# The keys' low part over all 128 rows of the array in the attention scores

## The chip, the cores and the metric

The kernel runs on one core of one Trainium2 chip. The metric is the device time of one execution in microseconds (us); the time before is 1739.68 us, the median of three runs (1738.67 to 1740.33). The engines are named as in the profile: PE multiplies matrices, PEld is its weight load (it loads the stationary operand, and overlaps PE), DVE is the vector engine, ACT the scalar engine, POOL the general-purpose engine, SP the engine that issues most transfers.

## The reference

The model is a two-layer transformer for 256 tokens of an image (a 4 by 64 grid) and 256 tokens of context, 1024 features, float32. Each layer has a half feed-forward, an attention block and a second half feed-forward, all modulated by a condition. The change lies in the attention's scores:

```
s_lat = einsum('bjqhd,bjykhd->bhjqyk', q_r, k_blk) * scale      # neighbourhood, 4 heads of 64
s_ctx = einsum('bjqhd,bchd->bhjqc', q_r, k_ctx) * scale         # the same queries on the context
p = softmax(concatenate([s_lat, s_ctx]))
...
s = einsum('bqkgd,bskd->bkgqs', q, k) * (64 ** -0.5)            # grouped heads: 8 of queries, 2 of keys
p = softmax(s); o = einsum('bkgqs,bskd->bqkgd', p, v)
```

In the first layer the context's tokens have their own queries, and attend to the context alone; in the second layer they only give keys and values.

## The kernel before, in words

All large products keep float32 accuracy by splitting each operand into a high part (float32r, which PE takes at its fast rate) and a low part, the remainder. `mm3` (L348, L349, L350) issues three matmuls for one product: high by high, high by low, low by high. These three lines are most of the program. Weights arrive by SP into `raw` buffers, ACT casts the high part (L306), DVE subtracts for the low part (L309), and both go into a buffer `w` of the pool `wp`, of which there are 7.

The order of all work is written out by hand: the kernel is traced under a manual schedule, and each engine runs its instructions in the order in which the code emits them. `later` and `tick` postpone small steps until so many microseconds of matmuls have been emitted. Buffers of a pool are handed out as earlier tiles are done with, and the framework adds the waits.

In `attention`, softmax goes by *units*. A unit is two heads: in a unit of kind "x", a block of 128 image tokens over all 512 keys; in a unit of kind "c", all 256 context tokens over the 256 context keys. The first layer has 4 + 8 units x and 2 + 4 units c (neighbourhood and grouped heads), the second 4 + 8 units x. `run` emits for each unit its scores, then dense matmuls that are independent of it (the amounts are in the table `FILL`), then the transposes of the unit two places earlier (`flip`, L878 and L883), so that DVE and ACT have time for the maximum (L855), the exponentials (L863) and the copies (L886).

A head has 64 features, and the array 128 rows, so the three terms of a score are packed into two matmuls. The queries' tile of two heads holds, for head i, the high part on that head's half of the rows and the low part on the other half. The keys' tile `K`, a buffer of the pool `wp`, has four planes of 512 columns: planes 0 and 1 are the high parts of heads 0 and 1, each on both halves of the rows; plane 2 has both low parts, head i on its half; plane 3 has the neighbourhood queries of the image tokens, in the spare room. The first matmul of a score (L838) is queries by high keys over all 128 rows, which sums two of the terms. The second (L839) is the third term, the queries' high part by the keys' low part, and uses only the 64 rows of head i:

```
PE.matmul(out=o, lhsT=q[:, i, tt * 128:(tt + 1) * 128], rhs=kt[:, i, keys], start=True, stop=False)
PE.matmul(out=o, lhsT=q[r, i, tt * 128:(tt + 1) * 128], rhs=kt[r, 2, keys], start=False, stop=True)
```

A unit x thus has four matmuls of 512 columns, which alternate between L838 and L839; a unit c has eight of 256 columns. `key_tile` allocates a tile K: two for the neighbourhood heads at the start of a layer's attention, one for the grouped heads before the third unit. `split_keys` fills it (ACT L710, DVE L713), `split_queries` fills the queries (ACT L724 or L721, DVE L725 or L722). The queries of later units lie in tiles `qst` of the pool tag `t2k`, of which there are 12; the probabilities `P`, the squares `qsq` and the pooling's matrices `pmd` share them. POOL does little here: the rotation's product (L736), and for the next layer a memset of `bm` and `pwbd` (L644, L645) and some gathers (L660).

Of the kernel before, what the change touches and what calls it, by code (L numbers as in the profile page):

```python
# [9 lines left out]
F32 = mybir.dt.float32  # L10
# [8 lines left out]
TX = 256  # L19
# [31 lines left out]
def dit_kernel(  # L51
# [123 lines left out]
    def ada_quantum(g, k, raw):  # L175
        """128 rows of two of the modulations, by the tensor engine."""
        if k == 0:
            ada_ps[g] = ps_ada.tile([128, 512], F32, tag="ada", name="ada")
        ps = ada_ps[g]
        for j in range(4):  # L180
            PE.matmul(out=ps[32 * j:32 * j + 32, :], lhsT=sc[:, k, :], rhs=raw[:, j * 512:(j + 1) * 512], start=(k == 0), stop=(k == KD - 1))  # L181
        st["raws"] -= 1
        loads()
        if k == KD - 1:
            sb = ada_rows(ada_ps.pop(g))
            later(5.0, lambda: ada_columns(sb, [2 * g, 2 * g + 1], 2))
# [3 lines left out]
    def conds(m):  # L190
        """How many conditions a modulation is for: the context's tokens end with the second layer's attention."""
        return 1 if m >= 14 else 2
# [8 lines left out]
    def ada_one():  # L201
        """The next block of the modulations, 128 rows by 512 columns, that the vector engine does: it sums both conditions'
        multiples of the rows; the sums over partitions are the tensor engine's, once for a modulation."""
# [38 lines left out]
    def ada_columns(sb, ms, n):  # L242
        """Rows 32j (and the one after) of four groups of columns become columns of the modulations ms."""
        tp = aux_bank()
        for q in range(2 * conds(ms[0]) if n == 1 else 4):
            PE.transpose(tp[:, q * 128:(q + 1) * 128], sb[:, q * 128:(q + 1) * 128], ident)
        tv = tp.rearrange("p (q j w) -> p q j w", q=4, j=4)
        for i, m in enumerate(ms):
            l, mod = divmod(m, 9)
            s = conds(m) if n == 1 else 2  # L250
            sl = modT[:, l * 72 + mod * 8:l * 72 + mod * 8 + 8, 0:s]
            if n == 1:
                v, o = tv[:, 0:2 * s, :, 0].rearrange("p (s q) j -> p j q s", s=s), sl.rearrange("p (j q) s -> p j q s", j=4)
            else:
                v, o = tv[:, :, 2 * i:2 * i + 2, 0:2].rearrange("p q j s -> p j q s"), sl.rearrange("p (j q) s -> p j q s", j=2)
            bsrc = (colsB if l else colsA)[:, mod * 8:mod * 8 + 8].rearrange("p (j q) -> p j q", j=o.shape[1])
            DVE.tensor_tensor(out=o, in0=v, in1=bsrc[:, :, :, None].to_broadcast(list(o.shape)), op=ALU.add)
            derived(l, mod, s)
# [12 lines left out]
    def next_main(force=False):  # L271
        """Whether the next weight block of the stream is on its way; ada blocks before it go to the tensor engine."""
# [7 lines left out]
    def run_ada():  # L280
        """Runs the next ada block of the stream, if that is what comes next."""
# [9 lines left out]
    def emit_split(between=None):  # L291
        """Splits the next slot of the stream into two float32r parts (ada blocks on the way go to the tensor engine)."""
# [51 lines left out]
    def mm3(ps, pairs, n, start, stop):  # L344
        """Accumulates products of split operands: pairs of ((wh, wl), (ah, al)); the first of each is stationary."""
# [17 lines left out]
    def acc_chunk(vs, k):  # L363
        """Squares of chunk k of the halves vs of the tokens; summed over chunks, but a half's last chunk apart."""
# [18 lines left out]
    def rsqrt(ps, n, scale):  # L383
        """1 / sqrt(ps * scale + EPS) of few elements, by Newton's steps from a guess at the exponent."""
# [27 lines left out]
    def spread(v, rb=None):  # L412
        """The tokens' factors on every partition."""
# [5 lines left out]
    def apply(v, i, a, pace=0.0, rb=None):  # L419
        """The operand of the next product: normed, scaled and shifted, in two parts."""  # L420
# [45 lines left out]
    def proj_out(src, kl, ppair, gate, both, final, after, each=None):  # L466
        """One part of a product into the residual. src(k) gives the moving operand; a slot has ppair chunks. In the final
        part the last two slots go by halves of the tokens, so that one half's norm runs under the other."""
# [35 lines left out]
    def boundary(i):  # L504
        """What follows a finished half: its statistic and its operand of the next product."""
# [26 lines left out]
    def by_halves(sl, a, both, evac):  # L532
        """Products of four slots, one half of the tokens after the other, chunk by chunk of the operand as it comes. Two
        products share a bank: the first start clears what the whole bank has had written."""
# [11 lines left out]
    def up_evac(pa, pb, g, m, nm, lo, hi):  # L546
        """g[m : m + nm] of the tokens lo:hi from the banks of both factors."""
# [89 lines left out]
    def attn_prep(l):  # L637
        """Bias of the neighbourhood's scores (masked), and the pooling weights as blocks of a diagonal."""
# [11 lines left out]
        # copies of a head's table at a pitch of 465, read back at a pitch of 464: row c starts c entries earlier  # L650
# [24 lines left out]
    def attention(l, a, both):  # L675
        """From the normed tokens to the operand of w_out and the first half of that product; both: the context's tokens
        are carried on too."""
# [20 lines left out]
        # k of the neighbourhood, k and v of the grouped heads: by halves of the tokens  # L698
        sl = [take() for _ in range(4)]

        def key_tile():
            """Keys of two heads: each one's high part on both halves of the rows, then both low parts; and some queries."""
            st["out"] += 1
            return wp.tile([128, 4, 512], F32R, tag="w", name="K")
        K = {("na", hp): key_tile() for hp in range(2)}

        def split_keys(kt, src, lo, hi):
# [3 lines left out]
            for i in range(2):  # L711
                r = slice(64 * i, 64 * i + 64)
                DVE.tensor_tensor(out=kt[r, 2, lo:hi], in0=src[r], in1=kt[r, i, lo:hi].bitcast(F32), op=ALU.subtract)  # L713

        def split_queries(dst, src, scale=None):
            """Queries of two heads, each one's high part on its half of the rows and its low part on the other."""
# [10 lines left out]
        def rotate(q, n):  # L727
            """Rotary embedding of n chunks of the first TX tokens in place."""
# [15 lines left out]
        def k_post():  # L744
            """Norm and rotation of the grouped heads' keys."""
# [29 lines left out]
        # q and v of the neighbourhood  # L775
        Q = {}
        for j in range(2):
# [3 lines left out]
            for v in halves(both):  # L781
                if v:
                    q = tmp.tile([128, 512], F32R, tag="t2k", bufs=T2K, name="qst")
                else:
                    q = K["na", j][:, 3]
# [18 lines left out]
        # the pooling's matrices: each block of tokens on itself; on its neighbour they are in k_edge  # L804
# [9 lines left out]
        def queries(br, kind, hs):  # L814
            """Both heads' queries as they are multiplied."""
# [7 lines left out]
        def scores(br, kind, hs, t):  # L823
            """x: one block of 128 tokens over all keys; c: all of the context's tokens over its keys."""
# [9 lines left out]
            for tt in ((t,) if br == "x" else (0, 1)):  # L834
                for i in range(2):
                    r = slice(64 * i, 64 * i + 64)
                    o = S[i] if br == "x" else S[i][:, tt * TX:(tt + 1) * TX]
                    PE.matmul(out=o, lhsT=q[:, i, tt * 128:(tt + 1) * 128], rhs=kt[:, i, keys], start=True, stop=False)  # L838
                    PE.matmul(out=o, lhsT=q[r, i, tt * 128:(tt + 1) * 128], rhs=kt[r, 2, keys], start=False, stop=True)  # L839
# [27 lines left out]
        def flip(br, kind, hs, t, Ps):  # L867
            """Probabilities with the keys on partitions; the products with v once a pair of heads has them all."""
# [59 lines left out]
        def run(jobs, fill, before):  # L928
            """Units of softmax, each one's probabilities turned depth units later."""
# [19 lines left out]
        def stat_col(c, tb):  # L949
            """Where the statistics of chunk c's two heads lie, for a block of tokens."""  # L950
            return c // 2 * nb * 4 + tb * 4 + c % 2 * 2

        def q_post(j):
            """Rotation and norm of two chunks of queries."""
# [9 lines left out]
        def rest_in():  # L964
            """q of the grouped heads and u of the pooling."""
# [27 lines left out]
        def rest_out():  # L993
            """The product with w_out's first half: the neighbourhood's and the pooling's chunks."""
# [53 lines left out]
        def piece():  # L1048
            """A piece of the work that is independent of the units."""
# [21 lines left out]
        def before(n):  # L1071
            """What the unit n needs, beyond its queries."""
# [40 lines left out]
    with tc.manual_schedule():  # L1113
        # small operands, laid in rows and turned into columns
# [13 lines left out]
        def quarter_load(h, i, raw):  # L1128
            """Half of the rows of the first shift's and scale's chunks 2h and 2h + 1."""
# [19 lines left out]
        def load_pair(v, k2):  # L1149
            """Two chunks of half the tokens, turned."""  # L1150
# [7 lines left out]
        def quarter_ada(h):  # L1158
            """The products of two chunks of the shift and scale: each of the array's four groups of columns sums a quarter of
            the rows."""  # L1160
# [25 lines left out]
        # sums of squares of the tokens as they come, a token on a partition  # L1186
# [27 lines left out]
        def first():  # L1214
            """The first four slots' products, as the shift and scale and with them the operand's chunks come."""
# [45 lines left out]
        def last_chunk(ch):  # L1261
            """A chunk of the result, scaled by the last norm's gains."""
# [20 lines left out]
        # final norm of the tokens, which are back in rows  # L1283
# [16 lines left out]
def _constants():  # L1300
    """Arrays that depend on the shapes alone."""
# [55 lines left out]
```

## Time and profile before

| what | value |
|---|---|
| median of 3 runs | 1739.68 us (1738.67 to 1740.33) |
| profiled execution: span from first to last instruction | 1741.7 us |
| PE busy | 1706.1 us, 98% |
| PE weight loads busy | 1428.7 us, 82% |
| DVE, ACT, POOL busy | 1025.0, 664.8, 33.3 us |
| mean granted clock of PE | 0.987 |
| L838 | 48 matmuls of 128x512, 24 of 128x256 |
| L839 | 48 of 64x512, 24 of 64x256 |

The page gives no other time of the profiled execution than its span, which is 2.0 us above the median of the runs. Busy times of PE overlap, because matmuls are pipelined: a matmul's duration is not what it adds to the program. What it adds is the time from its start to the start of the next one, which the timeline gives. Shapes in the rows are written rows*columns of the stationary operand and rows x columns of the moving one: 64*128 64x512 is a matmul that uses 64 rows of the array.

### The profile page before, as it was taken

How to read it: one execution, taken by the hardware profiler on the slowest of the kernel's cores; microseconds unless marked ns; L12 is line 12 of the kernel's file. 1: busy time of each engine (PE TensorE's matmuls, PEld its weight loads, DVE VectorE, ACT ScalarE, POOL GpSimd, SP SyncE). 2: the span in 40 equal slices, each digit the busy share in tenths (PEclk: the TensorE clock that was granted, in tenths of full speed). 3: DMA queues.
4: the chain of work that ended last, by engine and by line, in shares of the span. 5: the costliest groups of instructions: out<-in, count | busy, mean ns of one | idle time of the engine just before them, and what ended most of it. 6: DMA issues, size and time to landing. Idle time of an engine off the chain costs nothing.

```text
span 1741.7 us, 23662 instructions
## 1 busy us (share of the span) xinstructions
PE 1706.1 (98%) x9512; PEld 1428.7 (82%) x9512; DVE 1025.0 (59%) x1748; ACT 664.8 (38%) x1087; POOL 33.3 (2%) x48
## 2 busy tenths in 40 slices
PE   6999999999999999999999999999999999989998
PEld 4778888889886688888888898888888987789998
DVE  5666676566545586666664466545433656565554
ACT  4431322324545644323333243223222356554443
POOL 0000200000000000000000000020000000000000
PEclk8999999999999999999999999999999999989999
DMA  9755555431304325544653335455533133546561
GB/s 316 207 175 168 155 179 173 151 121 49 109 25 160 107 73 168 164 140 140 192 152 122 92 88 183 150 160 174 146 97 97 49 110 146 169 133 205 164 201 50
DMA packets 295335, 246.48 MB, mean 142 GB/s; under 512 B 9377, under 2 KB 262442, under 8 KB 293176
## 3 DMA queue, kind: packets, MB, share of 16 engines
q1 hardware_dynamic: 292680, 241.30, 44.7%
q0 software_dynamic: 1088, 2.15, 0.5%
q8 instruction: 75, 1.23, 0.3%
q10 hardware_dynamic: 1456, 1.52, 0.3%
q14 instruction: 36, 0.29, 0.1%
HBM read 243.88 MB, written 2.00 MB: 141 GB/s over the span
## 4 chain that ended last, share of the span: by engine, by line
PE 90%; DVE 4%; DMA 2%; ACT 2%; issue 1%; SPq 0%; DVEq 0%; ACTq 0%
PE mm L348 27%; PE mm L350 27%; PE mm L349 27%; PE mm L839 2%; PE mm L912 1%; PE aux L878 1%; PE mm L838 1%; DVE w L309 1%; PE ada L181 1%; DMA ada_raw<-in_w_ada_dram 1%; DVE ada_acc L221 1%; PE ada L229 1%; DMA raw<-in_w_ada_dram 1%; ACT w L306 1%; PE aux L409 0%
## 5 line engine op out<-in xcount | busy, mean ns | idle before, releaser
L348 PE MATMUL mm<-act,w 128*128 128x512 f32 (+1 forms) x2592 | 913.0, 352 | 5.6 <-ACT act L437 3.3
L350 PE MATMUL mm<-act,w 128*128 128x512 f32 (+1 forms) x2592 | 904.2, 349 | 1.8 <-DVE w L309 1.8
L349 PE MATMUL mm<-act,w 128*128 128x512 f32 (+1 forms) x2592 | 904.5, 349 | 1.0 <-DVE act L431 0.9
L348 PEld LDWEIGHTS mm<-act,w 128*128 128x128 f32 x2592 | 494.1, 191 | 89.3 <-issue 19.4
L350 PEld LDWEIGHTS mm<-act,w 128*128 128x128 f32 x2592 | 494.0, 191 | 64.1 <-DVE w L309 2.4
L349 PEld LDWEIGHTS mm<-act,w 128*128 128x128 f32 x2592 | 494.3, 191 | 62.5 <-DVE act L431 1.7
L309 DVE TENSOR_TENSOR w<-raw,w 128x1024 fp32r<-128x1024 f32 (+1 forms) x312 | 371.0, 1198 | 245.6 <-ACT w L306 245.2
L306 ACT CAST w<-raw 128x1024 fp32r<-128x1024 f32 (+1 forms) x312 | 314.9, 1023 | 120.4 <-PE mm L350 93.6
L221 DVE SCALAR_TENSOR_TENSOR ada_acc<-ada_raw,sc,ada_acc 128x512 f32<-128x512 f32 x308 | 216.0, 746 | 47.9 <-DMA ada_raw<-in_w_ada_dram 24.7
L558 ACT CAST act<-gf 128x512 fp32r<-128x512 f32 (+1 forms) x87 | 49.7, 571 | 318.7 <-DVE gf L555 318.7
L461 DVE SCALAR_TENSOR_TENSOR hT<-mm,hgt,hT 128x256 f32<-128x256 f32 x168 | 75.1, 480 | 97.8 <-PE mm L350 97.6
L552 ACT ACTIVATE sil<-mm 128x512 f32<-128x512 f32 (+1 forms) x87 | 47.6, 547 | 214.8 <-PE mm L350 214.5
L555 DVE TENSOR_TENSOR gf<-sil,mm 128x512 f32<-128x512 f32 (+1 forms) x87 | 54.3, 625 | 94.0 <-PE mm L350 77.7
L559 DVE TENSOR_TENSOR act<-gf,act 128x512 fp32r<-128x512 f32 (+1 forms) x87 | 54.9, 631 | 55.5 <-ACT act L558 55.5
L374 ACT ACTIVATE sq<-hT 128x256 f32<-128x256 f32 (+1 forms) x52 | 25.5, 492 | 108.4 <-DVE hT L461 108.4
L437 ACT ACTIVATE act<-nt,modT 128x256 fp32r<-128x256 f32 x88 | 43.4, 507 | 49.3 <-DVE nt L436 49.2
L219 ACT ACTIVATE ada_acc<-ada_raw,sc 128x512 f32<-128x512 f32 x44 | 29.6, 718 | 47.4 <-DMA ada_raw<-in_w_ada_dram 36.7
L855 DVE TENSOR_REDUCE nm<-mm 128x1 f32<-128x512 f32 (+1 forms) x60 | 41.0, 686 | 7.9 <-PE mm L839 7.2
L863 ACT ACTIVATE P<-mm,nm,rq 128x512 f32<-128x512 f32 (+1 forms) x48 | 33.7, 707 | 22.3 <-DVE nm L860 21.0
L431 DVE SCALAR_TENSOR_TENSOR act<-nt,modT,act 128x256 fp32r<-128x256 f32 x88 | 41.3, 480 | 1.3 <-ACT act L437 1.3
L436 DVE SCALAR_TENSOR_TENSOR nt<-hT,gsc,aux 128x256 f32<-128x256 f32 x88 | 40.8, 476 | 1.8 <-PE aux L416 1.2
L886 ACT COPY PT<-aux 128x512 f32<-128x512 f32 x60 | 32.2, 588 | 16.9 <-PE aux L878 12.9
(154 smaller groups left out, 885.5 us busy)
## 6 DMA issues: line engine op xcount, KB each, us to landing
raw<-in_ffn_up_dram SPq DMA_DIRECT2D x172, 512.0 KB
ada_raw<-in_w_ada_dram SPq DMA_DIRECT2D x192, 256.0 KB
raw<-in_ffn_down_dram SPq DMA_DIRECT2D x32, 1024.0 KB
raw<-in_w_ada_dram SPq DMA_DIRECT2D x16, 1024.0 KB
raw<-in_ffn_down_dram SPq DMA_DIRECT2D x16, 768.0 KB
raw<-in_w_in_dram SPq DMA_DIRECT2D x10, 1024.0 KB
raw<-in_w_out_dram SPq DMA_DIRECT2D x8, 1024.0 KB
raw<-in_w_ada_dram SPq DMA_DIRECT2D x12, 512.0 KB
```

The costliest lines, as they stand in the source:

```text
L221: DVE.scalar_tensor_tensor(out=o, in0=raw, scalar=col, in1=o, op0=ALU.mult, op1=ALU.add)
L306: ACT.copy(out=wh, in_=sl)
L309: DVE.tensor_tensor(out=wl, in0=sl, in1=wh.bitcast(F32), op=ALU.subtract)
L348: PE.matmul(out=ps, lhsT=wh, rhs=ah, start=start and i == 0, stop=False)
L349: PE.matmul(out=ps, lhsT=wh, rhs=al, start=False, stop=False)
L350: PE.matmul(out=ps, lhsT=wl, rhs=ah, start=False, stop=stop and i == last)
L437: ACT.activation(out=acol(a, k, v * TX, v * TX + TX)[0], in_=t, func=AF.Identity, bias=modT[:, l * 72 + 3 * n * 8 + k, v:v + 1])
L461: DVE.scalar_tensor_tensor(out=hT[:, k, cols], in0=ps, scalar=gate[:, k, v:v + 1], in1=hT[:, k, cols], op0=ALU.mult, op1=ALU.add)
L552: ACT.activation(out=s[:, 0:n], in_=pa[:, 0:n], func=AF.Silu)
L555: DVE.tensor_tensor(out=u[:, 0:n], in0=s[:, 0:n], in1=pb[:, 0:n], op=ALU.mult)
L558: ACT.copy(out=gh, in_=uv)
L559: DVE.tensor_tensor(out=gl, in0=uv, in1=gh.bitcast(F32), op=ALU.subtract)
```

## The change

The keys' low parts get a plane each, planes 2 and 3 of the tile K: head i's low part on its half of the rows, zeros on the other half. The second matmul then runs over all 128 rows with the same stationary operand as the first; the other head's half of the rows holds this head's low queries, which meet zeros. POOL writes the zeros when the tile is allocated, two memsets of 64 rows by 512 columns for each of the three tiles of a layer. Since plane 3 is taken, the image tokens' neighbourhood queries move to tiles `qst` of the tag `t2k`. (The changed file also lost its comments; lines from 705 on are moved by up to four.)

```
         def key_tile():
             st["out"] += 1
-            return wp.tile([128, 4, 512], F32R, tag="w", name="K")
+            kt = wp.tile([128, 4, 512], F32R, tag="w", name="K")
+            for i in range(2):
+                POOL.memset(kt[64 - 64 * i:128 - 64 * i, 2 + i].bitcast(F32), 0.0)
+            return kt
...
                 r = slice(64 * i, 64 * i + 64)
-                DVE.tensor_tensor(out=kt[r, 2, lo:hi], in0=src[r], in1=kt[r, i, lo:hi].bitcast(F32), op=ALU.subtract)
+                DVE.tensor_tensor(out=kt[r, 2 + i, lo:hi], in0=src[r], in1=kt[r, i, lo:hi].bitcast(F32), op=ALU.subtract)
...
             for v in halves(both):
-                if v:
-                    q = tmp.tile([128, 512], F32R, tag="t2k", bufs=T2K, name="qst")
-                else:
-                    q = K["na", j][:, 3]
+                q = tmp.tile([128, 512], F32R, tag="t2k", bufs=T2K, name="qst")
...
-                    r = slice(64 * i, 64 * i + 64)
                     o = S[i] if br == "x" else S[i][:, tt * TX:(tt + 1) * TX]
                     PE.matmul(out=o, lhsT=q[:, i, tt * 128:(tt + 1) * 128], rhs=kt[:, i, keys], start=True, stop=False)
-                    PE.matmul(out=o, lhsT=q[r, i, tt * 128:(tt + 1) * 128], rhs=kt[r, 2, keys], start=False, stop=True)
+                    PE.matmul(out=o, lhsT=q[:, i, tt * 128:(tt + 1) * 128], rhs=kt[:, 2 + i, keys], start=False, stop=True)
```

The order of PE's instructions stays as it was. On PE, at the first unit of the first layer, the two orders differ as follows (rows with - are of before, rows with + of the changed kernel; in brackets stands what the instruction waits for):

```order
-L838 MATMUL mm<-K 128x512 [waits DVE_49,PE_49]
-L839 MATMUL mm<-K 128x512
-L838 MATMUL mm<-K 128x512 [waits Activation_49]
-L839 MATMUL mm<-K 128x512
+L838 MATMUL mm<-K,qst 128x512 [waits DVE_49,PE_49]
+L839 MATMUL mm<-K,qst 128x512 [waits Pool_49]
+L838 MATMUL mm<-K,qst 128x512 [waits Activation_49]
+L839 MATMUL mm<-K,qst 128x512 [waits Pool_49]
```

The queries come from `qst` now, and the first second-matmuls of each tile K wait for POOL's zeros. On POOL, around the first layer's attention and up to the second layer's `bm`, the order before is:

```order
L660 DMA braw<-tab 64x4x64 x16
L736 ISA
L736 TENSOR_TENSOR qkv<-qkv,rope 128x256
L736 TENSOR_TENSOR qkv<-qkv,rope 128x2x256 x2
L644 MEMSET bm 128x2048
```

and after the change, where L707 is the memset of the zeros and L740 the rotation's product of L736:

```order
L660 DMA braw<-tab 64x4x64 x16
L707 MEMSET K 64x512 x4
L740 ISA
L740 TENSOR_TENSOR qkv<-qkv,rope 128x256
L707 MEMSET K 64x512 x2
L740 TENSOR_TENSOR qkv<-qkv,rope 128x2x256 x2
L644 MEMSET bm 128x2048
```

Four memsets stand ahead of the rotation of the keys, and two ahead of the rotations of the queries.

## The prediction

> **What bounds the kernel now.** I read the page first, for the engine that bounds the whole, then the same by stage, then what PE waits for in the stages that the change touches, and last the timeline of single score units.
>
> ```profile
> PE 1706.1 (98%) x9512; PEld 1428.7 (82%) x9512; DVE 1025.0 (59%) x1748; ACT 664.8 (38%) x1087; POOL 33.3 (2%) x48
> PE 90%; DVE 4%; DMA 2%; ACT 2%; issue 1%; SPq 0%; DVEq 0%; ACTq 0%
> ```
>
> PE is busy for 98% of the span and carries 90% of the chain that ended last. The busy share alone is no proof, since matmul durations overlap, so I look at the two stretches that hold the score units, and at PE's waits in them (one answer for each stretch, engine and releaser, us in total, times, longest):
>
> ```profile
> 457.00:610.00 153.00, 152.52 (x880) 107.65 (x878) 78.07 (x192) 86.01 (x200) 4.64 (x4) 0.98 0.28 93
> 1424.00:1508.00 84.00, 83.54 (x582) 60.74 (x581) 51.24 (x122) 53.81 (x115) 2.61 (x2) 1.00 0.42 152
> PE aux L883 <- ACT PT L886: 0.5, 2, 0.2
> PE mm L838 <- ACT P L863: 0.4, 1, 0.4
> ```
>
> The columns of the first two rows are length, then busy time of PE, PEld, DVE, ACT and POOL, granted clock, DMA share and GB/s. In 237 us of units, PE waits 0.9 us. ACT, the next busiest, works 86.01 of 153 us and 53.81 of 84 us. So here a microsecond less on PE is a microsecond less of the program, until ACT or DVE is in the way.
>
> Now the units themselves. These rows are the start, the modelled duration and the shape of PE's matmuls at the first unit, with dense work on both sides:
>
> ```profile
> 457.73 0.40 PE L838 MATMUL mm<-K 128*128 128x512 f32 x1
> 458.06 0.50 PE L839 MATMUL mm<-K 64*128 64x512 f32 x1
> ...
> 459.34 0.50 PE L348 MATMUL mm<-act,w 128*128 128x512 f32 x1
> 459.68 0.40 PE L349 MATMUL mm<-act,w 128*128 128x512 f32 x1
> 459.92 0.40 PE L350 MATMUL mm<-act,w 128*128 128x512 f32 x1
> 460.15 0.40 PE L348 MATMUL mm<-act,w 128*128 128x512 f32 x1
> ```
>
> Between full-row matmuls of 512 columns the next starts 0.23 us later (459.92 to 460.15). Inside the unit, where 128 and 64 rows alternate, the first step takes 0.33 us, the other three 1.28 together (458.06 to 459.34), 0.43 each, and even the step after the return to full rows (459.34 to 459.68) takes 0.34. The weight loads tell why:
>
> ```profile
> 458.91 0.18 PEld L839 LDWEIGHTS mm<-K 64*128 64x128 f32 x1 [0.24 <-issue]
> 459.33 0.19 PEld L348 LDWEIGHTS mm<-act,w 128*128 128x128 f32 x1 [0.24 <-issue]
> 459.92 0.19 PEld L348 LDWEIGHTS mm<-act,w 128*128 128x128 f32 x1
> ```
>
> In the unit the loads start only as their own matmul does (458.91 and 459.33, after 0.24 us of idle), so each step is 0.24 plus 0.18; in the dense stream the load of 459.92 belongs to the matmul of 460.15 and runs beside the one before. Loads of 64 and of 128 rows cost the same, 0.18 and 0.19 us; what the change of the number of rows costs is that they are no longer hidden.
>
> **The change, part by part.** It removes all changes of the number of rows inside a unit. The counts:
>
> ```profile
> L839 PE MATMUL mm<-K,qst 64*128 64x512 f32 x32 | 15.8, 495 | 0.0
> L839 PE MATMUL mm<-K 64*128 64x512 f32 x16 | 7.9, 496 | 0.0
> L839 PE MATMUL mm<-K,qst 64*128 64x256 f32 x24 | 9.1, 381 | 0.0
> ```
>
> That is 48 of 512 columns, two in a unit x: 24 units. And 24 of 256 columns, four in a unit c: 6 units.
>
> *A unit x.* From its first matmul to the one after the return, the first unit takes 459.68 - 457.73 = 1.95 us for five steps. At the dense stream's step these are 5 x 0.23 = 1.15, a gain of 0.80. Most units follow transposes, after which a full-row matmul has one longer step too; its price stands at places where dense work follows transposes, and at another unit:
>
> ```profile
> 507.82 0.48 PE L838 MATMUL mm<-K,qst 128*128 128x512 f32 x1
> 509.51 0.39 PE L348 MATMUL mm<-w,act 128*128 128x256 f32 x1
> 509.74 0.28 PE L349 MATMUL mm<-w,act 128*128 128x256 f32 x1
> 582.77 0.48 PE L348 MATMUL mm<-act,w 128*128 128x512 f32 x1
> 583.09 0.39 PE L349 MATMUL mm<-act,w 128*128 128x512 f32 x1
> 404.39 0.36 PE L348 MATMUL mm<-act,w 128*128 128x256 f32 x1
> 404.59 0.28 PE L349 MATMUL mm<-act,w 128*128 128x256 f32 x1
> 404.71 0.28 PE L350 MATMUL mm<-act,w 128*128 128x256 f32 x1
> ```
>
> Now 509.74 - 507.82 = 1.92; later 0.32 (582.77 to 583.09) + 3 x 0.23 + 0.12 (404.59 to 404.71, the step of 256 columns) = 1.13, a gain of 0.79. I take 0.80 for each: 24 x 0.80 = 19.2 us.
>
> *A unit c* has eight steps and the one after the return:
>
> ```profile
> 489.12 0.36 PE L838 MATMUL mm<-K,qst 128*128 128x256 f32 x1
> 491.60 0.50 PE L348 MATMUL mm<-act,w 128*128 128x512 f32 x1
> 491.94 0.39 PE L349 MATMUL mm<-act,w 128*128 128x512 f32 x1
> ```
>
> Now 491.94 - 489.12 = 2.82; later 0.20 (404.39 to 404.59, after transposes) + 7 x 0.12 + 0.23 = 1.27, a gain of 1.55. Six units: 9.3 us.
>
> *Less* for units that are followed by matmuls of fewer columns (L1015 128*64, L181 128*32), which change the array's shape anyway; there are seven, the first and the last of them:
>
> ```profile
> 529.72 0.50 PE L839 MATMUL mm<-K,qst 64*128 64x512 f32 x1
> 530.15 0.65 PE L1015 MATMUL mm<-pmd,qkv 128*64 128x128 f32 x4
> ...
> 1490.05 1.06 PE L181 MATMUL ada<-raw,sc 128*32 128x512 f32 x8
> 544.10 0.39 PE L350 MATMUL mm<-act,w 128*128 128x512 f32 x1
> 544.42 1.06 PE L181 MATMUL ada<-raw,sc 128*32 128x512 f32 x8
> ```
>
> There the last step goes from 0.43 to 0.32 (544.10 to 544.42), a gain of 0.11 and not 0.20, and the 0.11 after the return isn't had: 7 x 0.2 = 1.4 us less. PE's sum is 19.2 + 9.3 - 1.4 = 27.1 us.
>
> *The zeros.* Twelve memsets of 64x512 on POOL. The nearest rows:
>
> ```profile
> L644 POOL MEMSET bm<- 128x2048 f32 x2 | 3.6, 1824 | 0.0
> L645 POOL MEMSET pwbd<- 128x256 f32 x2 | 0.7, 331 | 34.9 <-issue 34.9
> 436.57 1.73 POOL L736 TENSOR_TENSOR qkv<-qkv,rope 128x256 f32<-128x256 f32 x1 [245.15 <-ACT w L306]
> 480.30 1.30 POOL L736 TENSOR_TENSOR qkv<-qkv,rope 128x512 f32<-128x512 f32 x1 [42.01 <-PE aux L732]
> 468.49 2.51 ACT L710 CAST K<-qkv 64x512 fp32r<-64x512 f32 x4
> ```
>
> Between 0.33 and 1.82 us each; by its length near the first, say 0.6. The neighbourhood's four memsets stand ahead of the rotation of the keys at 436.57, in 245.15 us of POOL's idle time, and their zeros are first read at 457.73, 21 us behind that rotation. The tile of the grouped heads is the same buffer that ACT fills from 468.49 on, so POOL can have its zeros done by 472 at the dearer price, while POOL has 42.01 us of idle time before the rotation at 480.30, and the first unit that reads the zeros starts at 507.82. Cost zero; the cover is that idle time, and without it the rotation of the queries, and with it the grouped heads' units, would come up to 3.6 us later in each layer, two memsets at 1.82.
>
> *The moved queries and low keys* cost ACT and DVE the same instructions into another tile or plane. Two more of the 12 `t2k` tiles are held in each layer until the fourth unit, so later tiles get other buffers, and some instructions wait for other ones. The transposes that free a tile P are emitted two units behind its scores, before the next tile that could need its place, and PE's waits above show no shortage, so I cost this at nothing; the bounds are 0 and what the rival on `t2k` below gives.
>
> *What is late next.* The units come 0.8 us closer, ACT and DVE keep their work. The two waits of 0.9 us in all are ACT's; each can grow by about a unit's gain where ACT is not released earlier. I take 1.5 us off, with ends of 0 and 8 (ten of the second layer's twelve units giving back 0.8 each). The forecast is 27.1 - 1.5 = 25.6 us less: 1716.1 for this execution, whose span is 2.0 above the median of the runs, so 1714 for the median.
>
> **The rivals.** *The load stays exposed.* The second matmul has the same stationary operand as the first, yet would load it again; if a load over all rows couldn't run beside a matmul on the same rows, each step would stay 0.24 + 0.19, as now, and the time 1740. For it: L838 has full rows, and the step from L838 to L839 is as long as the one back. Against it: in the dense stream loads of the same shape do run beside, and L348 and L349 share their stationary operand just so; hence 4 in 100. The Trainium skill's page "TensorE: Matmul & The Clock Gate", section "Part 3: Packing small matmuls — row/col tiling", states this rule: a weight load overlaps matmuls in flight only when the row group differs. By that rule the change would gain nothing, and the dense stream's loads at 0.23 us a step contradict it here.
>
> *Softmax takes over.* In the second layer ACT would work 53.81 of about 75 us, 72%; if half of the gain turned into waits on ACT or DVE, the time would be 1740 - 13 = 1727. Against it stand only 0.9 us of waits now, and transposes two units behind. 8 in 100.
>
> *Slower: the crowded `t2k`.* With two tiles more in use, a new P or `qsq` tile may have to wait for the transposes of an older one, so that ACT stands still and the scores wait for their bank. It decides from 27/30 = 0.9 us a unit on, somewhat more than a unit x gains; at twice its gain, 1.6 us a unit, the time would be 1740 - 27 + 48 = 1761. Against it: the order of all instructions is unchanged, and each buffer is freed by an instruction emitted earlier. 4 in 100.
>
> **How the numbers follow.** The forecast has 84 in 100, with its own range of 1709 (no loss, and 3 us of slow clock less: it was granted at 0.98 in the first stretch) to 1722 (8 us given back). The two rivals beside it, 1727 and 1740, and the slower one hold 16, so the range stays 1709 to 1722. Within 0.2%, 3.5 us, which is about what a measurement can tell from no change, lies only the exposed load: same 0.04. Faster 0.92, slower 0.04.
>
> **What would show it.** Inside a unit L838 and L839 start 0.23 us apart (0.12 in units c), and the first dense step after a unit takes 0.23. The units' lengths fall from 1.60 to about 0.9 and from 2.48 to 1.04 us. POOL has twelve memsets, all long before the units that read them. PE's waits in the two stretches stay under 3 us. It would be wrong if the steps stay at 0.42, if L839 waits for POOL, or if PE's waits on ACT grow by tens of microseconds.

## The result, and the profile after

The changed kernel takes 1719.26 us (median of 4 runs, 1716.95 to 1720.09), the kernel before beside it 1740.01 us (4 runs, 1738.67 to 1741.38): a ratio of 0.9882, with the interval 0.9868 to 0.9896, or 20.7 us less. The forecast was 1714, in the range 1709 to 1722. Run again twice, on two occasions, the changed kernel took 1714.77 and 1715.66 us, against 1738.91 and 1739.68: 24.1 and 24.0 us less. What differs between these sets is how long PE's clock stood at one half; among all runs with a mean granted clock of 0.990 the medians are 1739.7 (12 runs) and 1715.6 (5 runs), with 0.991 they are 1738.7 (15) and 1714.8 (2), and with 0.988, which three of the first set's four runs had, 1742.3 (4) and 1719.3 (4). So at equal clock the change is worth 23 to 24 us.

The profiled execution took 1716.95 us, with a span of 1715.2. First the page's busy times, and its chain of work that ended last:

```profile
PE 1675.8 (98%) x9512; PEld 1420.5 (83%) x9512; DVE 1024.0 (60%) x1748; ACT 663.5 (39%) x1087; POOL 40.0 (2%) x60
PE 90%; DVE 4%; DMA 3%; ACT 2%; issue 1%; SPq 0%; DVEq 0%; ACTq 0%
```

PE issues as many matmuls as before, is busy for 30.3 us less and still bounds the program; POOL has twelve instructions more. Next the table by stretches, for those that hold the score units (start and end, length; busy time of PE, PEld, DVE, ACT, POOL; granted clock, DMA share, GB/s), and PE's waits on ACT and on the modulations' blocks in them (us in total, times, longest):

```profile
457.00:592.00 135.00, 134.21 (x892) 103.25 (x890) 78.97 (x196) 86.27 (x205) 5.71 (x6) 1.00 0.32 106
1403.00:1483.00 80.00, 77.00 (x590) 61.34 (x588) 51.75 (x123) 54.56 (x116) 3.63 (x4) 1.00 0.47 164
PE mm L838 <- ACT P L863: 1.3, 1, 1.3
PE ada L181 <- DMA raw<-in_w_ada_dram: 1.2, 1, 1.2
PE aux L883 <- ACT PT L886: 0.5, 2, 0.2
```

The waits in the units have grown from 0.9 to 3.0 us: a wait of 0.4 on ACT's exponentials has become 1.3, and one of 1.2 us on a transfer is new. Both are in the second layer. (A wait of L246, 0.24 us in both executions, is left out: it lies behind the last unit.) The first unit x and the first unit c by the timeline (start, duration, instruction):

```profile
457.94 0.40 PE L838 MATMUL mm<-K,qst 128*128 128x512 f32 x1
458.17 0.40 PE L839 MATMUL mm<-K,qst 128*128 128x512 f32 x1
458.41 0.39 PE L838 MATMUL mm<-K,qst 128*128 128x512 f32 x1
458.64 0.40 PE L839 MATMUL mm<-K,qst 128*128 128x512 f32 x1
458.87 0.39 PE L348 MATMUL mm<-act,w 128*128 128x512 f32 x1
459.10 0.39 PE L349 MATMUL mm<-act,w 128*128 128x512 f32 x1
...
486.08 0.36 PE L838 MATMUL mm<-K,qst 128*128 128x256 f32 x1
486.28 0.28 PE L839 MATMUL mm<-K,qst 128*128 128x256 f32 x1
486.40 0.28 PE L838 MATMUL mm<-K,qst 128*128 128x256 f32 x1
...
487.11 0.40 PE L348 MATMUL mm<-act,w 128*128 128x512 f32 x1
487.34 0.40 PE L349 MATMUL mm<-act,w 128*128 128x512 f32 x1
```

A step of 512 columns takes 0.23 us, in the unit as on entry into dense work (458.41 to 458.64 to 458.87 to 459.10), one of 256 columns 0.12. The unit x lasts 0.93 us (1.60 before), the unit c 1.03 (2.48 before). Two of the weight loads in that unit x:

```profile
458.18 0.19 PEld L838 LDWEIGHTS mm<-K,qst 128*128 128x128 f32 x1
458.41 0.19 PEld L839 LDWEIGHTS mm<-K,qst 128*128 128x128 f32 x1
```

The load of 458.18 is that of the matmul of 458.41 and runs beside the one of 458.17; no idle time stands ahead of it, where before stood 0.24. Finally POOL's zeros, as a group (least, median and longest duration in ns, then the first and the last start) and the two of the second layer that are near a unit (the first layer has two such, at 466.1 us):

```profile
L707 POOL MEMSET K<- x12: 518/520/523, 395.5 to 1408.1; 64x512 f32 x12
1407.56 1.09 POOL L707 MEMSET K<- 64x512 f32 x2 [21.79 <-PE mm L350]
```

POOL had stood idle for 21.79 us (7.1 in the first layer), and the trace lists nobody who waited for these instructions.

The profiled pair differ by 26.5 us. That is 2.5 us more than 24. Before's execution has two stretches at half clock that after's lacks, 6.8 us from 499.7 and 3.4 us from 1516.8, together 5.1 us of PE's work; against that, after's longest wait of L409 on DVE is 4.9 us where before's is 3.4. The two rows are the same stretch of time, before and after, and the third column from the end is the clock, 0.50 and 1.00:

```profile
499.70:506.50 6.80, 6.80 (x29) 6.44 (x29) 3.20 (x8) 1.93 (x8) 3.02 (x2) 0.50 0.05 20
499.70:506.50 6.80, 6.80 (x57) 6.62 (x56) 3.43 (x14) 3.72 (x9) 0.00 (x0) 1.00 0.01 2
```

### The profile page after: what moved, and what is told of

It is laid out like the page before. It is cut to its first block, busy times and chain, and to the rows that moved or that the text cites. A ratio compares the mean times of both kernels' runs of the same rounds, so it can differ in the third digit from the quotient of the medians.

```text
span 1715.2 us, 23680 instructions
## 1 busy us (share of the span) xinstructions
PE 1675.8 (98%) x9512; PEld 1420.5 (83%) x9512; DVE 1024.0 (60%) x1748; ACT 663.5 (39%) x1087; POOL 40.0 (2%) x60
## 4 chain that ended last, share of the span: by engine, by line
PE 90%; DVE 4%; DMA 3%; ACT 2%; issue 1%; SPq 0%; DVEq 0%; ACTq 0%
PE mm L348 27%; PE mm L350 27%; PE mm L349 27%; PE mm L912 1%; PE aux L878 1%; DVE w L309 1%; DMA raw<-in_w_ada_dram 1%; DMA ada_raw<-in_w_ada_dram 1%; PE ada L181 1%; PE mm L838 1%; PE mm L839 1%; DVE ada_acc L221 1%; PE ada L229 1%; ACT w L306 1%; PE aux L409 0%
## 5 line engine op out<-in xcount | busy, mean ns | idle before, releaser
L348 PE MATMUL mm<-act,w 128*128 128x512 f32 (+1 forms) x2592 | 910.4, 351 | 5.7 <-ACT act L437 3.3
L348 PEld LDWEIGHTS mm<-act,w 128*128 128x128 f32 x2592 | 493.2, 190 | 86.7 <-issue 15.9
L374 ACT ACTIVATE sq<-hT 128x256 f32<-128x256 f32 (+1 forms) x52 | 25.6, 492 | 108.5 <-DVE hT L461 108.5
L863 ACT ACTIVATE P<-mm,nm,rq 128x512 f32<-128x512 f32 (+1 forms) x48 | 33.7, 708 | 21.9 <-DVE nm L860 18.9
L660 POOL DMA_DIRECT2D braw<-tab x32 | 19.5, 619 | 780.7 <-DVE gf L555 604.3
```

Of the source, the lines that this page charges most:

```text
L348: PE.matmul(out=ps, lhsT=wh, rhs=ah, start=start and i == 0, stop=False)
```

## The experiments

Theory: what the change removes is the price of changing the number of rows in use, about 0.2 us at each change. Rivals for the gain: the other places of the operands (planes, `qst`, the wait of tiles on one another), the stationary operand that L838 and L839 now share, or a cheaper way for ACT and DVE. For the loss against the forecast: ACT's exponentials are late, or the second layer's transfers are.

### The changed kernel again

It has no edit; it is there for the spread and to see whether the waits are the kernel's or the run's.

> The changed kernel once more, in five rounds, to size the gain with the clock of each run beside it. If the profiled executions (1741.7 and 1715.2 us) differ from the medians because of windows at half clock (three in the body of the one, at 499.7, 1404.2 and 1516.8 us among others, fewer in the other), then the spans of these runs fall into steps of about 2 to 3.4 us with the mean clock (0.990 near 1715, 0.988 near 1718), and the gain of the medians is 20 to 24 us. If the profiled pair's 26.5 us is the usual gain and the four runs were chance, the median is 1713 to 1716.

Median 1714.77 us (4 runs, 1714.49 to 1717.81), before 1738.91 (17 runs), ratio 0.9869 (0.9854 to 0.9883). Outside the waits, unit lengths are the same to 0.02 us. The wait of 1.3 us on the exponential is there again; that of L181 on its transfer is 0.2 us, and in its place PE waits one unit later:

```profile
PE aux L878 <- ACT PT L886: 0.9, 1, 0.9
```

So the first of the two waits is the kernel's. The second moves between a transfer and ACT's copy of transposed probabilities. What the two units there last together is looked at below.

### The new planes and tiles, but 64 rows

```
-                    PE.matmul(out=o, lhsT=q[:, i, tt * 128:(tt + 1) * 128], rhs=kt[:, 2 + i, keys], start=False, stop=True)
+                    r = slice(64 * i, 64 * i + 64)
+                    PE.matmul(out=o, lhsT=q[r, i, tt * 128:(tt + 1) * 128], rhs=kt[r, 2 + i, keys], start=False, stop=True)
```

> The changed kernel with its tiles, planes, zeros and moved queries, but the second product again on 64 rows. Theory (a change of the number of rows leaves the next weight load unhidden): steps of 0.42 us in units x and 0.31 in units c return, and the time is that of before, 1740 plus or minus 2; PE's waits stay where they were. Rival (the new place of queries and low keys, or the buffers, made the gain): about 1719.

1740.28 us (12 runs), ratio 1.0012 (1.0002 to 1.0022): no gain. In the timeline of the first unit (the second product's line is L840 here) the old steps are back:

```profile
457.25 0.50 PE L840 MATMUL mm<-K,qst 64*128 64x512 f32 x1
457.68 0.49 PE L838 MATMUL mm<-K,qst 128*128 128x512 f32 x1
458.11 0.49 PE L840 MATMUL mm<-K,qst 64*128 64x512 f32 x1
458.53 0.50 PE L348 MATMUL mm<-act,w 128*128 128x512 f32 x1
```

0.43, 0.43 and 0.42 us. No unit differs by more than 0.03 us from its length before. The zeros, the planes and the moved queries together cost 0.3 to 3.8 us by the times, but nothing by the units, and nothing at equal clock (with 0.990 the medians are 1739.6 and 1739.7, with 0.988 they are 1742.4 and 1742.3); the whole gain comes from the number of rows of the matmul.

### Full rows in the units c alone

```
+                    r = slice(64 * i, 64 * i + 64) if br == "x" else slice(0, 128)
+                    PE.matmul(out=o, lhsT=q[r, i, tt * 128:(tt + 1) * 128], rhs=kt[r, 2 + i, keys], start=False, stop=True)
```

> The second product over all 128 rows in the six units c alone, on 64 rows in the 24 units x. Theory: units c last 1.03 us as in the changed kernel and units x 1.70 as before; the prediction's sum gave 9.1 of 27.1 us to units c, so the time is 1740 - 9 = 1731, or 1733 if the gain is scaled to the measured 20.7. Rival (the units lose their gain to waits somewhere, so the two parts don't add up): under 4 us of gain, 1736 to 1740.

1729.45 us (6 runs, 1728.01 to 1732.04), ratio 0.9953 (0.9939 to 0.9967), or 5.7 to 10.6 us less. Over the six units c, with the step behind each, the trace gives 9.1 us; over the units x 0.0. The rest of the 24.0 us that the units of the changed kernel give, 14.9 us, is that of the units x. In one timeline both kinds stand side by side:

```profile
484.21 0.50 PE L840 MATMUL mm<-K,qst 64*128 64x512 f32 x1
484.64 0.50 PE L838 MATMUL mm<-K,qst 128*128 128x512 f32 x1
...
488.99 0.28 PE L838 MATMUL mm<-K,qst 128*128 128x256 f32 x1
489.11 0.28 PE L840 MATMUL mm<-K,qst 128*128 128x256 f32 x1
```

0.43 us a step where the rows change, 0.12 (at 256 columns) where they don't. The wait on the exponential is 0.4 us here as before the change: it grows with what the units x gain.

### Another stationary operand for the second product

```
-                    PE.matmul(out=o, lhsT=q[:, i, tt * 128:(tt + 1) * 128], rhs=kt[:, 2 + i, keys], start=False, stop=True)
+                    PE.matmul(out=o, lhsT=q[:, i, (1 - tt) * 128:(2 - tt) * 128], rhs=kt[:, 2 + i, keys], start=False, stop=True)
```

The second term is here that of the other block of tokens. It tells whether the steps are short because both matmuls share their weights.

> The changed kernel, with the second product's stationary operand taken from the other block of 128 tokens: the low keys' term is that of other tokens, so it is left out of the scores. Number of rows as in the changed kernel, but no two matmuls of a unit in a row share the stationary operand. Theory (rows): steps stay at 0.23 and 0.12 us, and the time at 1719 plus or minus 2. Rival (the load is hidden, or left out, because both products have the same stationary operand): steps of 0.42 return, about 1740.

1717.18 us (4 runs, 1715.05 to 1717.91), ratio 0.9877 (0.9863 to 0.9891), and the steps are the same:

```profile
457.90 0.40 PE L839 MATMUL mm<-K,qst 128*128 128x512 f32 x1
458.13 0.40 PE L838 MATMUL mm<-K,qst 128*128 128x512 f32 x1
458.37 0.40 PE L839 MATMUL mm<-K,qst 128*128 128x512 f32 x1
```

So every step loads new weights over all rows, and the load is hidden all the same. The rule of the Trainium skill's page "TensorE: Matmul & The Clock Gate", section "Part 3: Packing small matmuls — row/col tiling", that a load overlaps only when the row group differs, is contradicted here at 0.23 us a step with 0.19 us of load in it.

### The same rows in pairs

The kernel before, with both heads' first products ahead of both second products, so that the rows change twice in a group of four matmuls instead of four times:

```
+                os = [S[i] if br == "x" else S[i][:, tt * TX:(tt + 1) * TX] for i in range(2)]
+                for i in range(2):
+                    PE.matmul(out=os[i], lhsT=q[:, i, tt * 128:(tt + 1) * 128], rhs=kt[:, i, keys], start=True, stop=False)
                 for i in range(2):
                     r = slice(64 * i, 64 * i + 64)
-                    o = S[i] if br == "x" else S[i][:, tt * TX:(tt + 1) * TX]
-                    PE.matmul(out=o, lhsT=q[:, i, tt * 128:(tt + 1) * 128], rhs=kt[:, i, keys], start=True, stop=False)
-                    PE.matmul(out=o, lhsT=q[r, i, tt * 128:(tt + 1) * 128], rhs=kt[r, 2, keys], start=False, stop=True)
+                    PE.matmul(out=os[i], lhsT=q[r, i, tt * 128:(tt + 1) * 128], rhs=kt[r, 2, keys], start=False, stop=True)
```

> The kernel before, with the four products of two heads in another order: both first products (128 rows), then both second ones (64 rows each, on the two halves of the array). Two changes of the number of rows in place of four. Theory (the change of shape costs, not the 64 rows): the steps 128 to 64 and 64 to 128 stay at 0.42 us (0.31 in units c), the step between the two 64-row matmuls, which share no row, is much below 0.42; if it is near 0.01, as between matmuls on different columns of the array in the pooling, a unit x is 0.55 to 0.6 us shorter than before and a unit c about 1.0, together some 19 us: about 1720. Rival (every 64-row matmul has its load unhidden): steps of 0.42 between them too, a gain of about 7 us: 1732.

1721.78 us (6 runs, 1717.70 to 1723.53) against 1738.5 (11 runs), ratio 0.9897 (0.9881 to 0.9913). The first unit, where L837 is the first product, L840 the second, and a row of x2 stands for two matmuls:

```profile
457.18 0.64 PE L837 MATMUL mm<-K 128*128 128x512 f32 x2
457.75 0.50 PE L840 MATMUL mm<-K 64*128 64x512 f32 x2
458.18 0.50 PE L348 MATMUL mm<-act,w 128*128 128x512 f32 x1
458.52 0.40 PE L349 MATMUL mm<-act,w 128*128 128x512 f32 x1
```

Two matmuls of 64 rows, each of 0.50 us, together last 0.50: on different halves of the rows they start 0.003 us apart. The way back still costs 0.43 us and the step behind it 0.34 (458.18 to 458.52). From 128 to 64 rows the step is 0.33 us (0.57 less the 0.24 between the two L837), where 0.42 was expected from the kernel before.

The steps of both kernels fit one sum. A dense step is 0.23 us; it is 0.33 where the next matmul has another number of rows, 0.34 where the one before had, and 0.43 where both hold, as for a lone matmul between two changes. So the kernel before starts its first unit with a step of 0.33 (457.73 to 458.06), has three of 0.43, and the one after the return takes 0.34. Each change costs 0.2 us, half of it in the step ahead and half in the step behind; what each half consists of is not shown.

Some 70% of the gain is had without any zeros. By this sum, two changes fewer make 0.4 of the 0.60 us that the first unit gains, and the two matmuls side by side the rest.

### All score matmuls on 64 rows

The kernel before with `q[r, i, ...]` and `kt[r, i, keys]` in L838 too. The queries' low part by the high keys is left out.

> The kernel before, with the first product on 64 rows as well: the queries' low part by high keys is left out of the scores. Inside a head both matmuls have the same 64 rows, between heads the half changes, and only at a unit's ends does the number of rows. Theory (change of shape): within a head the step is 0.23 us (0.12 in units c), as in full-row streams. Rival (a load of 64 rows is never hidden): 0.42 (0.31) there too. If the heads overlap as well, a unit x lasts under 1 us.

One run: 1712.21 us. The first unit:

```profile
456.37 0.50 PE L838 MATMUL mm<-K 64*128 64x512 f32 x2
456.70 0.40 PE L839 MATMUL mm<-K 64*128 64x512 f32 x2
457.03 0.51 PE L348 MATMUL mm<-act,w 128*128 128x512 f32 x1
```

The unit lasts 0.66 us, and no step of 0.42 is left in it. Both heads run side by side: the second head's L838 starts 0.006 us after the first's, though the first head's L839 stands between them in the program. So 64 rows are not slow in themselves: what was slow is their alternation with 128. The two steps of 0.33 are longer than the dense 0.23 since one lies behind a change and the other ahead of one; at 256 columns, where steps lie between, those take 0.12 (484.70 to 484.82). The third term, which this kernel lacks, would need a third pair, by estimate another 0.23 us (the dense step), which brings the unit to 0.9 us, the length with zeros.

### More dense work between the second layer's first units

On the changed kernel, the first number of the second layer's row in `FILL` from 3.3 to 4.8, to give ACT time for the exponential on which the second unit waits.

> The changed kernel with more dense work behind the second layer's first unit (4.8 us in place of 3.3, of work that otherwise comes later). The theory says that part of the gain went back into a wait of L838 on ACT's exponential (L863) in the second unit of that layer, since ACT is not released earlier when units come closer: 1.3 us. With the wait filled it is under 0.3 us, and the time 1 us under the changed kernel at equal clock. Rival: the wait moves to the next unit, and nothing is gained.

1724.70 us (6 runs, 1722.96 to 1726.26), ratio 0.9918 (0.9903 to 0.9934), which is above the ratios of the changed kernel (0.9882, 0.9869 and 0.9867 in its three sets): slower by 6 to 9 us. L838's wait is gone from the list, and in its place stand

```profile
PE mm L985 <- DVE rs_v L388: 3.1, 1, 3.1
PE aux L878 <- ACT PT L886: 2.3, 1, 2.3
```

The dense work taken forward is missing further on, where the units' transposes and the queries' norms now come too early. The two waits are 5.4 us. With three smaller ones that are new (L1015 and L985, 1.7 us) and without that of L838, PE waits 5.7 us longer in the units than in the changed kernel's first profile. Two stretches at half clock also lie among the second layer's units of this run, where the other profiles have none (the third column from the end):

```profile
1423.00:1426.00 3.00, 3.00 (x17) 3.00 (x16) 0.84 (x5) 0.75 (x2) 0.00 (x0) 0.52 0.00 0
1453.60:1457.00 3.40, 3.40 (x19) 1.94 (x20) 0.00 (x0) 1.88 (x5) 0.00 (x0) 0.54 0.00 0
```

They take 3.4 us of PE's work there, but the mean granted clock is 0.990, as in the changed kernel's profile, which has more half clock further on; so they don't explain the loss. The rival was right and the loss larger than it said; whether the added dense work moves the half clock to this place is open.

### The exponentials' table loaded early

ACT's timeline in the changed kernel shows what the second unit waits for: the first exponential of the layer is preceded by the load of its table, which begins only when DVE's maximum is there. PE's row is that of the second unit's second head:

```profile
1408.56 1.28 ACT L863 ACT_TABLE_LOAD   x1 [2.59 <-DVE nm L855]
1410.68 0.50 PE L838 MATMUL mm<-K,qst 128*128 128x512 f32 x1 [1.33 <-ACT P L863]
```

The edit, in `soft`, on the changed kernel and on the kernel before; `warm` is a list made anew in each layer:

```
             P = tmp.tile([128, 512], F32, tag="t2k", bufs=T2K, name="P")
+            if not warm:
+                warm.append(small.tile([128, 8], F32, tag="warm", bufs=1, name="warm"))
+                ACT.activation(out=warm[0][:, 0:2], in_=colsB[:, 96:98], func=AF.Exp)
```

> The changed kernel, and ACT evaluates an exponential of 128x2 elements in each layer just ahead of the first unit's softmax, so that the table for the exponentials (1.28 us, ACT_TABLE_LOAD at L863, in the changed kernel at 1408.56, after 2.59 us of idle) is loaded in that idle time. Theory: this load is the longest of the waits that took from the gain. In the second layer the second unit's second head waits 1.33 us for the first unit's exponential, which could begin at about 1408.5 without the load and be done at 1409.4; the head's first matmul would start at 1409.2. So that wait falls to 0.1 to 0.3 us, the unit from 2.52 to about 1.2, and the program by 1.0 to 1.3 us against the changed kernel on the same chip. In the first layer PE didn't wait there, so nothing. Rival: the wait moves on, as with more dense work between the first two units; then the time stays or rises and PE's waits on ACT or DVE further on grow by about 1 us.

> The kernel before with the same early exponential. Theory: before the change the units were long enough to cover most of the load; only 0.36 us of wait stood there, so the program gains at most 0.4 us, which is no difference that the times can tell. Rival: the load costs 1.3 us in any kernel, since ACT is late throughout; then 1.3 us less.

> The changed kernel again, as the one to compare with on this chip: 1714 to 1719 us, and the wait of the second head on the first unit's exponential 1.3 us as before.

| kernel, same chip | median us | runs | ratio to before (1739.68, 15 runs) |
|---|---|---|---|
| changed | 1715.66 | 4, 1714.80 to 1718.65 | 0.9867 (0.9853 to 0.9880) |
| changed, early table | 1714.09 | 4, 1712.58 to 1716.13 | 0.9852 (0.9837 to 0.9867) |
| before, early table | 1738.08 | 11, 1735.29 to 1740.51 | 0.9992 (0.9983 to 1.0001) |

ACT's timeline and PE's row with the early table (the load's line is L856, the exponential's L867, the first product's L839):

```profile
1405.72 1.28 ACT L856 ACT_TABLE_LOAD   x1
1407.01 0.20 ACT L856 ACTIVATE warm<-colsB 128x2 f32<-128x2 f32 x1
1408.31 0.69 ACT L867 ACTIVATE P<-mm,nm 128x512 f32<-128x512 f32 x1 [1.10 <-DVE nm L859]
1409.14 0.50 PE L839 MATMUL mm<-K,qst 128*128 128x512 f32 x1
```

The load lies in ACT's idle time, the second unit lasts 1.24 us instead of 2.52, and the wait on the exponential is gone from the list, though this unit is still 0.3 us longer than the ones beside it (0.93). From the layer's first unit to its last the kernel takes 67.96 us instead of 69.07 on the same chip, 1.1 less: the theory's size, and the wait didn't move on. The times of the two agree with that but don't prove it, since their intervals overlap. For the kernel before the table costs no more than the interval, 0 to 3 us; its wait of 0.4 us is gone from the list too. So the table's load was nearly hidden before, and the change uncovered it. By its median the changed kernel with the early table is the fastest of those run that leave nothing out, but not by more than the spread.

The two units that share their loss last 2.35 and 1.06 us in the first profile of the changed kernel, 1.34 and 2.06 in the second, 2.02 and 1.38 in the third, 1.67 and 1.73 with the early table: 3.40 or 3.41 each time, as against 3.39 before the change. Whatever the transfer for L181 does in the first of them, the two together last as long; the wait for ACT's copies (L886) in the second profile points to these as what ends last, which no run tested by itself.

## Why the prediction was right

Time, range and sign came out; the sum of the units is 24.0 us where 25.6 was forecast. By its steps:

*Steps inside a unit*: right. 0.23 and 0.12 us, loads hidden, no idle time ahead of them. That the rows' change costs this, and not the load as such, is shown by the layout alone (no gain), the other stationary operand (full gain) and the 64 rows throughout (no 0.42). The prediction's account of a step, 0.24 us and an exposed load of 0.18, gives the length of the middle steps but not those of 0.33 and 0.34; by the paired run the price goes with the change of rows, half ahead of it and half behind. The Trainium skill's page "TensorEngine Tiling (Array Packing)", section "Tiling Modes", says that changing the tiling mode drains the engine, and that tiles work in parallel. The trace agrees: 0.42 against 0.23 us, and two matmuls 0.003 us apart.

*Units x, 24 x 0.80 = 19.2*: the fifteen that nothing held, and that no narrow matmuls follow, gain 0.77 to 0.80, 0.79 on the mean, which is 18.9 for 24. *Units c, 6 x 1.55 = 9.3*: 1.55, right. *Seven units with narrow followers, 0.2 less each*: five units x gain 0.58 to 0.60 and one c 1.35, right to 0.02; the seventh, at 1465.1 of before, was held.

*Waits, 1.5 us*: this is the term that was mis-sized. What held the units took 2.8. The unit at 1430.2 of before gained -0.38 instead of 0.79, since the 1.28 us of table load behind DVE's maximum had been covered, but for 0.36, by the unit's own length. The two at 1465.1 and 1468.6 gained -0.66 and 0.64, nothing together where 1.4 us were forecast. And the one at 1477.5 gained 0.54: its last step in the changed kernel is 0.37 us (L839 at 1454.95, L348 at 1455.32), and L348 starts 0.05 us behind the end of ACT's sum of the exponentials, which points to ACT. No list of waits has this one, since PE counts as busy in it. "Each can grow by about a unit's gain" was the right size for one unit; four units were held, not two. The table load stood in ACT's timeline of before, with the same 2.59 us of idle time ahead of it, and PE waited for the exponential behind it, so it could have been priced:

```profile
1429.22 1.28 ACT L863 ACT_TABLE_LOAD   x1 [2.59 <-DVE nm L855]
1431.35 0.50 PE L838 MATMUL mm<-K 128*128 128x512 f32 x1 [0.36 <-ACT P L863]
```

Then 18.9 + 9.3 - 1.4 - 2.8 = 24.0, as summed over the units.

*Zeros at nothing*: right. 0.52 us each (0.6 said), and nobody waits. *Moved queries and low keys at nothing*: right; with the new tiles alone no unit changes by more than 0.03 us, so the rival of the crowded `t2k` falls. The rival of the load that stays exposed falls by the steps of 0.23 us. *Softmax takes over* holds in two of thirty units, for 1.4 of 27 us; in the pair that lost another 1.4, a transfer's part and ACT's are not told apart.

*The median*: 1719.26 in the first set is 5 us above the forecast, 1714.77 and 1715.66 in the others are 1 to 2 above. The spread between sets goes with the clock: three of the first set's four runs had 0.988, and most of the others 0.990 or 0.991.

## What to carry to other kernels

Price a matmul by the step to its neighbour, not by the rows it uses: a matmul of 64 rows between matmuls of 128 cost 0.2 us more on the way there and as much on the way back, so that zeros over the other half made it cheaper; where zeros have no room, putting the two 64-row matmuls side by side gave 70% of that. When PE's work between two stages gets shorter, look at the first instruction of each function on ACT: a table load that was covered may not be, and an early small activation in idle time takes it away.

## What was not expected of the hardware

Matmuls on different halves of the rows run side by side, even past one that stands between them in the program: 0.003 and 0.006 us apart. The table load takes 1.28 us in either place, and, loaded early, the next activation starts 0.01 us behind its end (1405.72 + 1.28 to 1407.01). A change between 128 and 64 rows costs half ahead of it and half behind. PE's half clock comes in stretches that shift from run to run, of 6.8 us in the stretch shown above; one such stretch is 3.4 us of PE's work, as much as the bound of 0.2% that a measurement of this kernel can tell.
